# Start of a hybrid decoder block: how x is loaded, prepared and squared, and when the side work begins

## The chip, the core and the metric

The kernel runs on one core of a Trainium2 chip. The metric is the time of one execution in microseconds (us), as the device measures it; the median of several executions is compared. The core's engines are TensorE (PE, with its weight loads PEld), VectorE (DVE), ScalarE (ACT), GpSimd (POOL) and SyncE (SP); each works through its own list of instructions in order, and they wait for one another by semaphores. DMA transfers are issued by SP or ACT.

## What is computed

One decoder layer on 256 positions of width 2048, in fp32. What matters here is the beginning:

```python
h = rms_norm(x, g_mix)                 # x: (256, 2048)
proj = h @ w_in                        # 2048 x 8272; its columns are u, z_ssm, c_q, k, v, z_attn, ...
y_ssm = s5_branch(u, ...) * silu(z_ssm)  # S5: a scan over positions, on tables made from a, b, c, dt
...                                    # attention branch, gated merge, output projection, final norm
```

The row factor of the norm is taken out of the product: `proj = rstd * ((x * g_mix) @ w_in)`. So the products can start before the sum of squares of x is known, and the factor (`row1`) is applied when the sums are read from PSUM.

## The kernel before

**Units.** All weights come in 256 units of 128 x 1024 floats or less (512 KB). For each unit SP loads `raw` (5 buffers), ACT rounds it to `hi` (`unit_hi`, L252, 4 buffers), DVE takes `lo = raw - hi` (`unit_lo`, L264, 4 buffers), and PE multiplies: hi by the high part of the activations, hi by their low part, lo by their high part. A unit of the first 32 holds 8 blocks of 128 x 128 and makes 24 products of 256 columns. Units 0 to 3 are the first two blocks of u, woven: the first halves of both (x blocks 0 to 7), then the second halves (x blocks 8 to 15). They add up in one `aux` tile of PSUM, later blocks in `main` tiles (3 buffers).

**x.** x is loaded transposed, 16 blocks of 128 x 256 floats (2 MB), into `xT` (tile S). For each block ACT makes the high part (`xgh`, tile XH, L360) and DVE the low part (`xgl`, tile XL, L362). GpSimd squares blocks 0 to 7 and adds up most of the squares (L364, L368 to L370), ACT squares blocks 8 to 15 in one instruction (L367), DVE does the last two additions (L372, L373). From them come `rstd_cols` and `row1`.

**The main loop.** Step s issues the products of unit s on PE, then `unit_hi(s + 3)`, what was deferred to this step, `unit_lo(s + 2)`, the load of a further unit, and then `pump(1.3)`: the side work (generators, with costs in us) may spend 1.3 a step; what is not spent is kept up to 3.0. A generator that yields `("lag", n)` rests n steps. The framework then orders each engine's instructions by the order in the code and by an estimate of when they are ready, so an instruction may run somewhat before those written ahead of it.

**Side work of S5.** `s5_tables` (spawned with a lag of 3 steps) makes tables on DVE, GpSimd and PE. `s5_gen` starts when u (step 16) and the tables are there, and goes through two halves. Each half copies its input E from PSUM (ACT, L846), runs a long chain of DVE instructions on it (`cmadd`, L859 to L865), and at the end makes its output on PE (tile `aux`, 32 to 128 columns each). The first unit of c_q (step 104) has `need=["s5"]`: what is left of `s5_gen` is written out there, ahead of that unit's products. Steps 32 to 63 and 80 to 103 are units of 12 products of 512 columns, the others up to 104 of 24 products of 256.

**Beginning.** `first_loads` puts the gains, x and units 0 to 4 in one order on SP's queue. 18 products on a tile of zeros (`warm`) follow on PE. The first ACT instruction (`first`, L138) stands before all of this.

Of the kernel before, what the change touches and what calls it, by code (L numbers as in the profile page):

```python
# [12 lines left out]
AF = mybir.ActivationFunctionType  # L13
ALU = mybir.AluOpType
# [4 lines left out]
P = 128  # L19
T = 256  # L20
# [8 lines left out]
GA1 = 3  # L29
NC = 4  # L30
CW = 512
NWARM = 18
BUDGET = 1.3
XLAG = 1
ULATE = 4
TRLAG = 2

C_U, C_ZS, C_CQ, C_K, C_V, C_ZA, C_KI, C_GS, C_GA = 0, 1024, 2048, 2560, 2816, 3072, 4096, 4176, 6224
# [6 lines left out]
def block_kernel(ctx: ExitStack, tc: tile.TileContext, A: dict, out: bass.AP):  # L45
    nc = tc.nc
    V, S, G, PE = nc.vector, nc.scalar, nc.gpsimd, nc.tensor
    TT, STT = nc.vector.tensor_tensor, nc.vector.scalar_tensor_tensor
# [11 lines left out]
    def nm(s):  # L60
        uid[0] += 1
        return f"{s}_{uid[0]}"

    def slot(tag, shape, dt=F32):
        return cp.tile(shape, dt, tag=tag, name=nm(tag))

    def const(s, shape, dt=F32):
        return cp.tile(shape, dt, tag=s, name=s)
# [7 lines left out]
    def aux_ps():  # L76
        return pa.tile([P, 2, 512], F32, tag="aux", name=nm("aux"))
# [10 lines left out]
    def issue_unit(between=None):  # L88
        n = dma_next[0]
        if n >= len(units):  # L90
            return
        c, h, cols = units[n][:3]
        kind, idx = chunks[c]
        r = wp.tile([P, 1024], F32, tag="raw", name=nm("raw"), bufs=5)
        src = (A["wts"][idx] if kind == "w" else A["wvk"][idx])[:, h * cols:(h + 1) * cols]
        q = 2 if between else 1
        for i in range(q):
            s = slice(i * cols // q, (i + 1) * cols // q)
            nc.sync.dma_start(r[:, s], src[:, s])
            if between and i == 0:  # L100
                between()
        raws[n] = r
        dma_next[0] += 1
# [4 lines left out]
    gains = const("gains", [P, N_GAIN])  # L108
    xT = slot("S1", [P, KT, T])
    sabc = const("sabc", [P, 3, 32])  # L110

    def first_loads():
        def xload(k, n):
            nc.sync.dma_start(xT[:, k:k + n, :], A["xT"][:, k:k + n, :])

        nc.sync.dma_start(gains, A["gains"])
        xload(0, 2)
        issue_unit(lambda: xload(2, 2))
        xload(4, 4)
        issue_unit()  # L120
        xload(8, 4)
        xload(12, 4)
        for i in range(3):
            issue_unit()
        nc.sync.dma_start(sabc, A["sabc"])

    def gcol(base, i, p0=0, p1=P):
        return gains[p0:p1, base + i:base + i + 1]
# [6 lines left out]
    mhalf = const("mhalf", [P, 2])  # L135
    V.memset(mhalf, -0.5)
    first = const("first", [P, 2])
    S.activation(first, mhalf, AF.Copy)  # L138


    def mm(o, l, r, start=True, stop=True, **kw):
        PE.matmul(o, l, r, start=start, stop=stop, **kw)  # L142

    def mm3(o, wh, wl, ah, al, start, stop):
        mm(o, wh, ah, start=start, stop=False)
        mm(o, wh, al, start=False, stop=False)
        mm(o, wl, ah, start=False, stop=stop)
# [4 lines left out]
    def rstd_cols(sq, n, denom, tag, more=None):  # L152
        v = cp.tile([P, 2], F32, tag=tag + "_v", name=tag + "_v")
        if more is None:
            ps = small_ps()
            for t in range(2):
                mm(ps[:, 2 * t:2 * t + 2], sq[:n, t * P:(t + 1) * P], ones[:n, :])
            ss = ps[:, 0:4:2]
        else:
            ps = aux_ps()  # L160
            for m in (sq, more):
                for t in range(2):
                    mm(ps[:, t, 0:2], m[:n, t * P:(t + 1) * P], ones[:n, :], start=m is sq, stop=m is more)
            ss = ps[:, :, 0]
        V.tensor_scalar(v, ss, 1.0 / denom, EPS, ALU.mult, ALU.add)
        col = cp.tile([P, 2], F32, tag=tag + "_c", name=tag + "_c")
        G.tensor_tensor(col, v, mhalf, ALU.pow)
        return col
# [22 lines left out]
    def defer(n, fn):  # L191
        deferred.append((step[0] + n, fn))
# [14 lines left out]
    def spawn(gen, lag=0):  # L207
        t = [gen, step[0] + lag, False]
        threads.append(t)
        return t  # L210

    def spawn_first(gen):
        t = spawn(gen)
        threads.insert(0, threads.pop())
        return t
# [21 lines left out]
    def drain(t):  # L237
        while not t[2]:
            advance(t)
# [3 lines left out]
    def unit_hi(u):  # L243
        if u >= len(units):
            return
        cols = units[u][2]
        hi = wp.tile([P, 1024], F32R, tag="hi", name=nm("hi"))
        src = raws[u][:, :cols]
        q = 2 if u < 3 else 1
        for i in range(q):  # L250
            o = slice(i * cols // q, (i + 1) * cols // q)
            S.copy(hi[:, o], src[:, o])  # L252
        his[u] = hi
# [13 lines left out]
    def add_chunk(u0, u1, cols=1024, idx=None):  # L267
        c = len(chunks)
        if idx is None:
            n = sum(1 for k in chunks if k[0] == "w")  # L270
            chunks.append(("w", n))
        else:
            chunks.append(("v", idx))
        units.append((c, 0, cols) + u0)
        units.append((c, 1, cols) + u1)
# [1 line left out]
    def flush():  # L277
        run_deferred(True)

    def block_k16(act, evac, need=None, need1=None, M=P, acc=None, late=1):  # L280
        st = {}

        def go(h, hi, lo):
            ah, al = act()
            if h == 0:
                st["ps"] = (acc or main_ps)()
            ps = st["ps"]
            for k in range(8):
                kt = 8 * h + k
                mm3(ps[:M, :T], hi[:, k * M:(k + 1) * M], lo[:, k * M:(k + 1) * M], ah[:, kt, :], al[:, kt, :],  # L290
                    kt == 0, kt == 15)
            if h == 1:
                defer(late, lambda: evac(ps))
        return (lambda hi, lo: go(0, hi, lo), need), (lambda hi, lo: go(1, hi, lo), need1)
# [46 lines left out]
    R = {}  # L341
# [12 lines left out]

    xsq = slot("S2", [P, KT, T])

    def xprep(q):
        r = slice(4 * q, 4 * q + 4)
        for k in range(4 * q, 4 * q + 4):
            S.activation(xgh[:, k, :], xT[:, k, :], AF.Copy, scale=gcol(G_MIX, k))  # L360
        for k in range(4 * q, 4 * q + 4):
            STT(xgl[:, k, :], xT[:, k, :], gcol(G_MIX, k), xgh[:, k, :].bitcast(F32), ALU.mult, ALU.subtract)  # L362
        if q < 2:
            G.tensor_tensor(xsq[:, r, :], xT[:, r, :], xT[:, r, :], ALU.mult)  # L364

    def xnorm_gen():
        S.activation(xsq[:, 8:16, :], xT[:, 8:16, :], AF.Square)  # L367
        G.tensor_tensor(xsq[:, 0:4, :], xsq[:, 0:4, :], xsq[:, 4:8, :], ALU.add)  # L368
        G.tensor_tensor(xsq[:, 8:12, :], xsq[:, 8:12, :], xsq[:, 12:16, :], ALU.add)
        G.tensor_tensor(xsq[:, 0:4, :], xsq[:, 0:4, :], xsq[:, 8:12, :], ALU.add)  # L370
        yield ("lag", XLAG)
        TT(xsq[:, 0:2, :], xsq[:, 0:2, :], xsq[:, 2:4, :], ALU.add)  # L372
        TT(xsq[:, 0, :], xsq[:, 0, :], xsq[:, 1, :], ALU.add)  # L373
        yield 1.0
        yield ("lag", 1)
        R["col1"] = rstd_cols(xsq[:, 0, :], P, D, "r1")
        yield ("lag", 1)
        R["row1"] = row_of(R["col1"], "row1")
# [7 lines left out]
    def ev_u(nb):  # L386
        def f(ps):
            drain(R["xnorm"])
            TT(u[:, nb, :].rearrange("p (r j m) -> p r j m", r=2, j=4),
               ps[:, :T].rearrange("p (m j r) -> p r j m", j=4, r=2),  # L390
               R["row1"].rearrange("p (m j r) -> p r j m", j=4, r=2), ALU.mult)
            if nb == 7:
                R["s5"] = spawn(s5_gen(), 1)
        return f

    def late_x():
        xprep(2)
        xprep(3)
        R["xnorm"] = spawn_first(xnorm_gen())

    ua = {}

    def first_acc(nb):
        def f():
            if nb == 0:
                ua["ps"] = aux_ps()
            return ua["ps"][:, nb, :]
        return f

    for nb in range(8):  # L410
        first = nb < 2
        add_chunk(*block_k16(xact, ev_u(nb), need1=[late_x] if nb == 0 else None,
                             acc=first_acc(nb) if first else None, late=ULATE if first else 1))
        if nb == 1:
            weave()

# [671 lines left out]
    assert sum(1 for c in chunks if c[0] == "w") == NCH, (len(chunks), NCH)  # L1088


    R["s5t"] = spawn(s5_tables(), 3)
    first_loads()
    for i in range(NWARM):
        mm(wps[:, :T], warm[:, :P], warm)
    unit_hi(0)
    xprep(0)
    unit_lo(0)
    xprep(1)
    unit_hi(1)
    unit_lo(1)  # L1100
    unit_hi(2)
    NU = len(units)
    for s in range(NU):
        step[0] = s
        fn, need = units[s][3:]
# [129 lines left out]
```

## Time and profile before

| | us |
|---|---|
| median of 3 runs (lowest to highest) | 811.97 (811.44 to 812.96) |
| the profiled execution | 811.61 |
| its span, first to last instruction | 809.8 |
| PE busy in the span | 783.5 (97%) |
| DVE busy | 575.1 (71%) |
| ACT busy | 393.9 (49%) |
| GpSimd busy | 72.7 (9%) |

Times in the rows below are us from the start of the span, durations us if not marked ns. An engine that was idle carries in brackets how long it was, and what ended the wait. The granted clock (PEclk) is 1.00 at 2.4 GHz and 0.50 at 1.2 GHz.

### The profile page before, as it was taken

The numbers are of one execution on the slowest core, as the hardware profiler recorded it, in microseconds if no ns is written. First come the engines' busy times: TensorE is split into PE (matmuls) and PEld (weight loads), VectorE is DVE, ScalarE is ACT, GpSimd is POOL, SyncE is SP. The second block draws the span as 40 slices with busy tenths as digits, with TensorE's granted clock in tenths as the row PEclk, the third lists the DMA queues.
The fourth block names the chain that finished last, engine by engine and source line by source line (L and its number), as shares of the span: only waits on it lengthen the run. The fifth ranks groups of instructions, "written<-read, shape, count | busy, mean of one in ns | idle before, by whom it ended". The sixth has DMA issues, their size and how long they took to land.

```text
span 809.8 us, 12802 instructions
## 1 busy us (share of the span) xinstructions
PE 783.5 (97%) x5020; PEld 676.5 (84%) x5020; DVE 575.1 (71%) x834; ACT 393.9 (49%) x536; POOL 72.7 (9%) x77
## 2 busy tenths in 40 slices
PE   6899999999999999999999999999999999999993
PEld 5899997887999887799999987887887888888882
DVE  6999656999645999664669877666688555556662
ACT  6354544544566454463445474535445444445542
POOL 4369900000000000000000000000000000000000
PEclk7999999999999999999999999999999999999997
DMA  8576854656745655734754546676767665555522
GB/s 288 182 261 193 270 192 141 201 177 210 260 135 176 194 184 182 252 121 129 243 183 156 194 162 226 224 238 199 268 202 236 224 204 185 184 182 181 184 79 104
DMA packets 52061, 158.07 MB, mean 195 GB/s; under 512 B 5920, under 2 KB 12064, under 8 KB 51616
## 3 DMA queue, kind: packets, MB, share of 16 engines
q1 hardware_dynamic: 47392, 150.96, 57.2%
q10 hardware_dynamic: 4608, 6.29, 2.2%
q8 instruction: 39, 0.64, 0.3%
q14 instruction: 22, 0.18, 0.1%
HBM read 147.79 MB, written 8.39 MB: 193 GB/s over the span
## 4 chain that ended last, share of the span: by engine, by line
PE 36%; issue 11%; DMA 1%; DVE 1%; ACT 1%; ACTq 0%; POOLq 0%; POOL 0%; DVEq 0%
PE main L142 33%; PE aux L142 2%; PE aux L150 1%; DMA zld<-za_d 1%; DVE lo L264 0%; ACT hi L252 0%; DMA raw<-in_wts_dram 0%; DVE S L1022 0%; ACT S L1127 0%; ACTq L1230 0%; ACT S L586 0%; DVE t L980 0%; POOLq L1230 0%; POOL r_c L633 0%; ACT S L1023 0%
## 5 line engine op out<-in xcount | busy, mean ns | idle before, releaser
L252 ACT CAST hi<-raw 128x1024 fp32r<-128x1024 f32 (+2 forms) x259 | 266.4, 1031 | 363.7 <-PE main L142 318.3
L264 DVE TENSOR_TENSOR lo<-raw,hi 128x1024 fp32r<-128x1024 f32 (+2 forms) x259 | 316.5, 1225 | 154.6 <-ACT hi L252 154.0
L142 PE MATMUL main<-hi,S 128*128 128x512 f32 x544 | 175.3, 397 | 0.9 <-ACT S L1023 0.9
L142 PE MATMUL main<-hi,XH 128*128 128x512 f32 (+1 forms) x416 | 163.1, 392 | 0.0
L142 PE MATMUL main<-lo,XH 128*128 128x512 f32 (+1 forms) x416 | 162.4, 390 | 0.4 <-DVE lo L264 0.4
L142 PE MATMUL main<-hi,XL 128*128 128x512 f32 (+1 forms) x416 | 161.9, 389 | 0.0
L142 PE MATMUL main<-XH,hi 128*128 128x256 f32 x448 | 127.5, 285 | 0.0
L142 PE MATMUL main<-XH,lo 128*128 128x256 f32 x448 | 126.2, 282 | 0.0
L142 PE MATMUL main<-XL,hi 128*128 128x256 f32 x448 | 126.1, 282 | 0.0
L142 PEld LDWEIGHTS main<-hi,S 128*128 128x128 f32 x544 | 102.2, 188 | 25.2 <-ACT S L1023 1.6
L142 PE MATMUL main<-lo,S 128*128 128x512 f32 x272 | 107.9, 397 | 0.0
L142 PEld LDWEIGHTS main<-lo,XH 128*128 128x128 f32 x416 | 78.1, 188 | 18.8 <-DVE lo L264 1.9
L142 PEld LDWEIGHTS main<-hi,XH 128*128 128x128 f32 x416 | 78.1, 188 | 18.0
L142 PEld LDWEIGHTS main<-hi,XL 128*128 128x128 f32 x416 | 78.1, 188 | 17.3
L142 PEld LDWEIGHTS main<-XH,hi 128*128 128x128 f32 x448 | 84.8, 189 | 0.6
L142 PEld LDWEIGHTS main<-XH,lo 128*128 128x128 f32 x448 | 84.8, 189 | 0.0
L142 PEld LDWEIGHTS main<-XL,hi 128*128 128x128 f32 x448 | 84.7, 189 | 0.0
L142 PE MATMUL main<-S,hi 128*128 128x256 f32 x384 | 69.3, 283 | 0.1
L142 PEld LDWEIGHTS main<-S,hi 128*128 128x128 f32 x384 | 58.9, 188 | 1.7 <-issue 1.0
L142 PEld LDWEIGHTS main<-lo,S 128*128 128x128 f32 x272 | 51.2, 188 | 11.0
L142 PE MATMUL main<-S,lo 128*128 128x256 f32 x192 | 53.8, 280 | 0.0
L142 PEld LDWEIGHTS main<-S,lo 128*128 128x128 f32 x192 | 36.2, 188 | 0.0
(213 smaller groups left out, 687.0 us busy)
## 6 DMA issues: line engine op xcount, KB each, us to landing
raw<-in_wts_dram SPq DMA_DIRECT2D x247, 512.0 KB, 4.0
raw<-in_wvk_dram SPq DMA_DIRECT2D x8, 336.0 KB, 2.9
gs_d<-big ACTq DMA_DIRECT2D x8, 256.0 KB, 3.9
ga_d<-big ACTq DMA_DIRECT2D x8, 256.0 KB, 4.0
big<-gs_d SPq DMA_DIRECT2D x8, 256.0 KB, 4.3
big<-ga_d SPq DMA_DIRECT2D x8, 256.0 KB, 3.8
S<-in_grow_dram SPq DMA_DIRECT2D x2, 1024.0 KB, 7.7
big<-in_xtok_dram SPq DMA_DIRECT2D x8, 256.0 KB, 3.9
```

Of the source, the lines that this page charges most:

```text
L142: PE.matmul(o, l, r, start=start, stop=stop, **kw)
L150: PE.matmul(o, i, idn, is_transpose=True)
L252: S.copy(hi[:, o], src[:, o])
L264: TT(lo[:, o], src[:, o], his[u][:, o].bitcast(F32), ALU.subtract)
```

## The change

- x and the gains are loaded on ACT's queue, in order, and no longer between the units on SP's. Units 0 to 4 stand alone on SP's queue; two further units are issued ahead of the loop, so that the loop issues unit s + 7.
- GpSimd no longer works on x. ACT squares x in two instructions of 8 blocks (steps 2 and 3 of the loop), DVE adds all squares up (additions of 8, 4, 2 and 1 blocks, steps 4 and 5).
- The first two blocks (units 0 to 3) go by pass: 8 products of hi and high x, 8 of lo and high x, 8 of hi and low x, where each x block had its three products together.
- x is prepared in two groups of 8 blocks ahead of the loop; blocks 8 to 15 were prepared in step 2.
- 30 products on zeros in place of 18. The instruction `first` comes behind the loads.
- The first four blocks of u are read from PSUM later (6, 5, 3 and 2 steps after their last unit in place of 4, 4, 1 and 1).
- `xnorm_gen` is spawned ahead of the loop with a lag of 2; `s5_tables` starts with a lag of 7 steps in place of 3.

```diff
-NWARM = 18
+NWARM = 30
...
-            nc.sync.dma_start(xT[:, k:k + n, :], A["xT"][:, k:k + n, :])
-
-        nc.sync.dma_start(gains, A["gains"])
+            nc.scalar.dma_start(xT[:, k:k + n, :], A["xT"][:, k:k + n, :])
+
+        nc.scalar.dma_start(gains, A["gains"])
         xload(0, 2)
-        issue_unit(lambda: xload(2, 2))
+        xload(2, 2)
         xload(4, 4)
-        issue_unit()
         xload(8, 4)
         xload(12, 4)
-        for i in range(3):
+        issue_unit(lambda: None)
+        for i in range(4):
             issue_unit()
         nc.sync.dma_start(sabc, A["sabc"])
...
-            for k in range(8):
+            if split:
+                for i, (w, a) in enumerate(((hi, ah), (lo, ah), (hi, al))):
+                    for k in range(8):
+                        kt = 8 * h + k
+                        mm(ps[:M, :T], w[:, k * M:(k + 1) * M], a[:, kt, :], start=kt == 0 and i == 0,
+                           stop=kt == 15 and i == 2)
+            for k in range(0 if split else 8):
...
     def xnorm_gen():
-        S.activation(xsq[:, 8:16, :], xT[:, 8:16, :], AF.Square)
-        G.tensor_tensor(xsq[:, 0:4, :], xsq[:, 0:4, :], xsq[:, 4:8, :], ALU.add)
-        G.tensor_tensor(xsq[:, 8:12, :], xsq[:, 8:12, :], xsq[:, 12:16, :], ALU.add)
-        G.tensor_tensor(xsq[:, 0:4, :], xsq[:, 0:4, :], xsq[:, 8:12, :], ALU.add)
-        yield ("lag", XLAG)
-        TT(xsq[:, 0:2, :], xsq[:, 0:2, :], xsq[:, 2:4, :], ALU.add)
-        TT(xsq[:, 0, :], xsq[:, 0, :], xsq[:, 1, :], ALU.add)
-        yield 1.0
+        for h in range(2):
+            S.activation(xsq[:, 8 * h:8 * h + 8, :], xT[:, 8 * h:8 * h + 8, :], AF.Square)
+            yield ("lag", 1)
+        for n in (8, 4, 2, 1):
+            TT(xsq[:, 0:n, :], xsq[:, 0:n, :], xsq[:, n:2 * n, :], ALU.add)
+            yield 1.0
         yield ("lag", 1)
...
-        first = nb < 2
-        add_chunk(*block_k16(xact, ev_u(nb), need1=[late_x] if nb == 0 else None,
-                             acc=first_acc(nb) if first else None, late=ULATE if first else 1))
+        add_chunk(*block_k16(xact, ev_u(nb), acc=first_acc(nb) if nb < 2 else None,
+                             late=(6, 5, 3, 2)[nb] if nb < 4 else 1, split=nb < 2))
...
-    R["s5t"] = spawn(s5_tables(), 3)
+    R["xnorm"] = spawn(xnorm_gen(), 2)
+    R["s5t"] = spawn(s5_tables(), 7)
     first_loads()
+    S.activation(first, mhalf, AF.Copy)
     for i in range(NWARM):
         mm(wps[:, :T], warm[:, :P], warm)
     unit_hi(0)
-    xprep(0)
+    xhi(range(8))
     unit_lo(0)
-    xprep(1)
+    xlo(range(8))
     unit_hi(1)
     unit_lo(1)
     unit_hi(2)
+    xhi(range(8, 16))
+    xlo(range(8, 16))
+    for i in range(2):
+        issue_unit()
```

## Rows read from the trace of the kernel before

**Rows 1.** The page, busy time by engine: us, share of the span, instructions

```profile
PE 783.5 (97%) x5020; PEld 676.5 (84%) x5020; DVE 575.1 (71%) x834; ACT 393.9 (49%) x536; POOL 72.7 (9%) x77
```

**Rows 2.** Timeline of PE, 0 to 45: start, us, what [idle before <-releaser]

```profile
1.04 4.02 PE L142 MATMUL main<-warm 128*128 128x256 bf16 x18 [1.04 <-DVE mhalf L136]
...
15.32 0.58 PE L142 MATMUL aux<-XL,hi 128*128 128x256 f32 x1 [1.49 <-DVE XL L362]
...
24.15 0.27 PE L142 MATMUL main<-XL,hi 128*128 128x256 f32 x1
27.52 0.39 PE L142 MATMUL aux<-XH,lo 128*128 128x256 f32 x1 [3.09 <-DVE lo L264]
...
31.11 0.42 PE L142 MATMUL aux<-XH,lo 128*128 128x256 f32 x1
31.32 0.41 PE L142 MATMUL main<-XH,lo 128*128 128x256 f32 x1
...
32.33 0.28 PE L142 MATMUL main<-XL,hi 128*128 128x256 f32 x1
...
33.75 0.28 PE L142 MATMUL main<-XL,hi 128*128 128x256 f32 x1
```

**Rows 3.** Windows: stretch, busy us by engine (instructions), then PEclk, DMA share, GB/s

```profile
8.36:18.59 10.23, 6.30 (x24) 5.42 (x25) 8.88 (x13) 8.67 (x18) 4.33 (x3) 0.50 0.95 355
...
28.84:32.25 3.41, 3.41 (x19) 3.41 (x18) 3.15 (x6) 0.90 (x1) 0.00 (x0) 0.50 0.83 267
...
10.00:15.00 5.00, 1.74 (x5) 1.01 (x4) 4.56 (x3) 4.45 (x11) 4.31 (x2) 0.50 1.01 392
```

**Rows 4.** Timeline of DVE, 0 to 45

```profile
11.09 4.97 DVE L362 SCALAR_TENSOR_TENSOR XL<-S,gains,XH 128x256 fp32r<-128x256 f32 x4 [0.44 <-ACT XH L360]
...
17.19 3.24 DVE L362 SCALAR_TENSOR_TENSOR XL<-S,gains,XH 128x256 fp32r<-128x256 f32 x8
...
24.08 4.52 DVE L264 TENSOR_TENSOR lo<-raw,hi 128x1024 fp32r<-128x1024 f32 x2
...
29.12 1.21 DVE L264 TENSOR_TENSOR lo<-raw,hi 128x1024 fp32r<-128x1024 f32 x1
```

**Rows 5.** Timeline of GpSimd, 0 to 45

```profile
10.59 1.89 POOL L364 TENSOR_TENSOR S<-S 128x1024 f32<-128x1024 f32 x1 [2.22 <-DMA S<-in_xT_dram]
...
19.40 4.51 POOL L369 TENSOR_TENSOR S<-S 128x1024 f32<-128x1024 f32 x1 [4.42 <-ACT S L367]
```

**Rows 6.** Timeline of ACT, 0 to 45

```profile
0.72 1.28 ACT L138 ACT_TABLE_LOAD   x1 [0.72 <-PEq L1224]
...
13.19 3.30 ACT L360 ACTIVATE XH<-S,gains 128x256 fp32r<-128x256 f32 x8
...
17.42 1.91 ACT L367 ACTIVATE S<-S 128x2048 f32<-128x2048 f32 x1
```

**Rows 7.** Timeline of SP's queue, 0 to 45

```profile
3.06 0.43 SPq L114 DMA_DIRECT2D S<-in_xT_dram  x1
3.53 0.43 SPq L99 DMA_DIRECT2D raw<-in_wts_dram  x1
```

**Rows 8.** DMA issues at 3.06 and 3.53: count, KB, us from issue to landing

```profile
S<-in_xT_dram SPq DMA_DIRECT2D x1, 512.0 KB, 7.5
...
raw<-in_wts_dram SPq DMA_DIRECT2D x1, 512.0 KB, 8.3
```

**Rows 9.** Timeline of DVE: begin and end of the second S5 half's chain

```profile
259.45 1.23 DVE L859 TENSOR_TENSOR S<-S,pre 128x1024 f32<-128x1024 f32 x1 [0.57 <-ACT S L846]
...
331.80 4.83 DVE L264 TENSOR_TENSOR lo<-raw,hi 128x1024 fp32r<-128x1024 f32 x4
```

**Rows 10.** Windows: the stretch of that chain, columns as in rows 3

```profile
260.00:330.00 70.00, 69.79 (x338) 57.42 (x337) 69.21 (x100) 30.89 (x32) 0.00 (x0) 1.00 0.58 189
```

**Rows 11.** Timeline of PE: that half's input (E), and its output at step 104

```profile
256.58 1.16 PE L142 MATMUL aux<-S,S 64*128 64x128 f32 x16
...
337.02 0.64 PE L142 MATMUL aux<-S,S 128*32 128x128 f32 x16
```

More of the change, by code (lines that the diff above doesn't have):

```diff
@@ L31 @@
 CW = 512
-NWARM = 18
+NWARM = 30
 BUDGET = 1.3
-XLAG = 1
-ULATE = 4
 TRLAG = 2
@@ L137, in block_kernel @@
     first = const("first", [P, 2])
-    S.activation(first, mhalf, AF.Copy)
     def mm(o, l, r, start=True, stop=True, **kw):
@@ L278, in flush, with block_k16 @@
         run_deferred(True)
-    def block_k16(act, evac, need=None, need1=None, M=P, acc=None, late=1):
+    def block_k16(act, evac, need=None, need1=None, M=P, acc=None, late=1, split=False):
         st = {}
@@ L355, in block_kernel, with xhi, xlo @@
     xsq = slot("S2", [P, KT, T])
-    def xprep(q):
-        r = slice(4 * q, 4 * q + 4)
-        for k in range(4 * q, 4 * q + 4):
+    def xhi(ks):
+        for k in ks:
             S.activation(xgh[:, k, :], xT[:, k, :], AF.Copy, scale=gcol(G_MIX, k))
-        for k in range(4 * q, 4 * q + 4):
+    def xlo(ks):
+        for k in ks:
             STT(xgl[:, k, :], xT[:, k, :], gcol(G_MIX, k), xgh[:, k, :].bitcast(F32), ALU.mult, ALU.subtract)
-        if q < 2:
-            G.tensor_tensor(xsq[:, r, :], xT[:, r, :], xT[:, r, :], ALU.mult)
     def xnorm_gen():
-        S.activation(xsq[:, 8:16, :], xT[:, 8:16, :], AF.Square)
-        G.tensor_tensor(xsq[:, 0:4, :], xsq[:, 0:4, :], xsq[:, 4:8, :], ALU.add)
-        G.tensor_tensor(xsq[:, 8:12, :], xsq[:, 8:12, :], xsq[:, 12:16, :], ALU.add)
-        G.tensor_tensor(xsq[:, 0:4, :], xsq[:, 0:4, :], xsq[:, 8:12, :], ALU.add)
-        yield ("lag", XLAG)
-        TT(xsq[:, 0:2, :], xsq[:, 0:2, :], xsq[:, 2:4, :], ALU.add)
-        TT(xsq[:, 0, :], xsq[:, 0, :], xsq[:, 1, :], ALU.add)
-        yield 1.0
+        for h in range(2):
[4 more added lines that the diff above has]
+            yield 1.0
         yield ("lag", 1)
@@ L394, in ev_u @@
         return f
[L396 to L399, printed above, removed]
     ua = {}
```

## The prediction, made before the result was known

> **What bounds the kernel now.** I read the page first: PE is busy for 97% of the span [rows 1], so only what makes PE idle or slow counts. Next the timeline of PE by idle time. The holes lie in the first 33 us, and in the tail after the last product, which the change doesn't touch. At the start PE stands again and again for x, the last time until 15.32, and once for 3.09 us on `lo` [rows 2]. The windows add a second loss: the granted clock is 0.50 (1.2 GHz) from 8.36 to 18.59 and from 28.84 to 32.25 [rows 3], each time behind a stretch in which PE had mostly stood; it rose at 18.59 after PE had run unbroken from 15.32.
>
> To put both losses in one number: at 32.33 the clock is high and the 104th real product begins (96 of units 0 to 3, over at 31.11; of the fifth unit two near 24.15 and five from 31.32). From there products begin (33.75 - 32.33) / 12 = 0.118 us apart [rows 2]. An unbroken run at that pace would have begun at 32.33 - 103 x 0.118 = 20.2. This is the start to beat.
>
> The timelines of DVE and GpSimd tell why `lo` was late: four XL beside GpSimd's squares took 4.97 us, where eight later ones took 3.24, and two `lo` beside its addition took 4.52, where one alone takes 1.21 [rows 4, 5].
>
> **The change part by part: the start.** x and weights go out on two queues at once. Of the first 2 MB (x blocks 0 to 7, units 0 and 1) before's order let x blocks 4 to 7 land at 3.06 + 7.5 = 10.56, and unit 1, the last of them, at 3.53 + 8.3 = 11.83 [rows 7, 8]. No row shows two queues loading together here, so these two are the bounds for x blocks 4 to 7: its old place, or an even share with the weights, which puts it at the end of the 2 MB. I take the middle, 11.2.
>
> The Trainium skill ("DMA: Bandwidth & Descriptors", section "Queues, rings and completion order") says that each DMA engine takes turns between the queues that have work, a packet at a time. By it 11.8 is right, x comes later than before and 0.6 us is lost against my sum; no run here shows it yet.
>
> On ACT six issues of some 0.45 (SP's took 0.43 [rows 7]) delay the table load of 1.28 [rows 6] from 0.72 to about 3.4, so ACT is free near 4.9. That is before most of x lands: hidden.
>
> ACT needs 3.30 / 8 = 0.41 for a block [rows 6], so blocks 4 to 7 end at 11.2 + 1.65 = 12.85, and the first pass of unit 0 with them. Its other 16 products then have their operands (XL at 3.24 / 8 = 0.40, now without GpSimd). The clock will be low again, because PE stands between the warm-up and 11.2; at 0.21 a product (31.11 to 31.32 [rows 2]) they take 3.4, to 16.25. By then PE has run unbroken for 3.4 us, as it had for 3.3 when the clock rose at 18.59. Unit 1 follows at full pace; its `hi` is ready near 14. That is 24 products at 16.25, a start of 16.25 - 24 x 0.118 = 13.4. **Gain: 20.2 - 13.4 = 6.8.** If x lands at 11.83 and the clock rises only at 18.6, it is 5.3. If it lands at 10.56 and the compiler fills the wait with second and third passes of blocks 0 to 3 (8 products, 1.7), it is 9.
>
> Later needs: unit 2 begins at 16.25 + 24 x 0.118 = 19.1. The second 2 MB at 392 GB/s [rows 3] land 5.1 after 11.2, at 16.3, and ACT's last four blocks are done at about 18.2. Just in time.
>
> Costs elsewhere: 12 more warm-up products follow 18 that took 4.02 [rows 2]; at 0.118 to 0.22 they end between 6.5 and 7.7, while PE still waits for x. ACT squares 8 more blocks (1.91 [rows 6]) and DVE adds 8 and 4 blocks more (1.21 for 1024 columns [rows 4], so at most 2.4 + 1.2 = 3.6). `lo` takes 1.21 of a unit's 2.84, so in steps 4 to 9 this and the readings of u fit, but the small S5 work slips behind them. The later readings of u hold no buffer that is missed: the third `main` buffer is free, and block 5, which reuses that of block 2, starts at step 10, two steps after it is read. The earlier units on SP's queue wait for the same buffers as before: nothing.
>
> **The change part by part: the tables.** They seem free, as they fill DVE's idle time, but they set when S5 reaches PE. I counted credits. Before, the tables start at step 3 with 3.0 saved, lose 1.0 to the squares, and need 23.7 up to the powers: 3.0 - 1.0 + 1.3 x 17 first reaches it in step 20. After, the squares take 4.0 in steps 4 and 5 and the start at step 7 finds 2.9: 2.9 + 1.3 x 16 = 23.7, step 23. All behind it is lags and the same budget, so every later piece comes 3 steps later: the last products of E of the second half in step 78, not 75.
>
> Before, those stand at 256.58 [rows 11], DVE's chain on them begins at 259.45, and the four `lo` behind its last instruction begin at 331.80 [rows 9]. In between DVE is busy for 69.21 of 70 us [rows 10], so the chain cannot be squeezed. PE takes up its result at 337.02, at step 104 [rows 11], which does not move. Slack: 5.2. Three units of 24 products are 3 x 2.84 = 8.5. So E comes 8.5 later against PE, and PE stands for **8.5 - 5.2 = 3.3** ahead of the output; behind it are the whole queue of PE and then `hi`, which waits for PE's buffers. From below: nothing, if the compiler lays unit 104's products ahead of the output. From above: three more `lo` inside the chain (3.6), and a low clock afterwards. From 28.84 to 32.25, behind the 3.09 us wait, this cost 3.41 / 0.21 = 16 products x 0.095 = 1.5 [rows 2, 3]. Together 8.4. I take 3.3, since both orders of the `lo` seen here keep the chain at its length.
>
> **Sum.** The profiled execution took 811.61: 811.61 - 6.8 + 3.3 = 808.1. The median of the runs is 0.36 above it: **808.5 us**.
>
> **The rivals.**
> *A, as above:* 6.8 gained, some 3 given back at step 104; 807 to 810.5. For it: the saturated chain. Against it: only the compiler's order.
> *B, nothing given back:* PE fills the wait with unit 104, or the chain comes in time; 811.97 - 6.8 = 805.2, with the start's upper bound 803. For it: at 24.15 the compiler had put two products of the fifth unit ahead of the fourth's [rows 2]. Against it: before, it had laid four `lo` behind the chain's end [rows 9], so it judged the output ready early.
> *C, the change does not do what it says at the start:* x gains no speed by a second queue, ACT's list stands behind the second half of unit 0, or XH of blocks 12 to 15 is late for unit 2. Then some 3 to 4 are gained and 3.3 given back: 811.5 to 812.3.
> *D, slower:* the same wait at step 104, with the `lo` of units 103 to 105 ahead of the chain's end and the clock low after it: 8.4 lost against 6.8, 813.6. It decides once the wait with its clock is over 6.8.
>
> **How the numbers follow.** A 0.45, B 0.27, C 0.18, D 0.10. The measurement tells about 0.2%, 1.6 us, from no change. Faster than 810.3: A but for 0.03, all of B, 0.03 of C: 0.72. Slower than 813.6: half of D, 0.01 of C, and 0.02 for a stall that I have not seen: 0.08. The same: 0.20. The range reaches from the middle of B to the middle of C: 804.4 to 812.0, which leaves out 0.04 of B, 0.05 of C and D.
>
> **What would show it.** Right: real products unbroken from about 13, the clock at 2.4 GHz from about 16, the 104th product near 13.4 + 103 x 0.118 = 25.6 in place of 32.33; no XL or `lo` above 1.3 in the first 40 us; near 330 a wait of PE of about 3 us in front of aux products, released by DVE's chain (L865), with E's last products 3 units later than before. Wrong: x blocks 4 to 7 after 12, a second low clock before 30, PE going on with c_q's first unit ahead of the S5 output (B), or any PE wait on `lo` in steps 4 to 10, where DVE has 3.6 us more to do.

## The result, and the profile of the changed kernel

The changed kernel took 818.7 us (median of 4 runs, 816.27 to 819.09) against 812.47 of before beside it: ratio **1.0069, 95% interval 1.0042 to 1.0095**. It is 0.7% slower; 808.5 was forecast. The profiled execution took 816.27 us, its span is 814.5. It is the shortest of the four: the other three took 818.5 to 819.1, at a mean granted clock of 0.981 to 0.983 against its 0.986.

The page of the changed kernel, busy time as in [rows 1], and all waits of PE above 3 us (total, times, longest):

```profile
PE 786.5 (97%) x5032; PEld 678.6 (83%) x5032; DVE 575.5 (71%) x836; ACT 398.0 (49%) x539; POOL 58.3 (7%) x72
```
```profile
PE main L139 <- DVE lo L261: 5.1, 3, 4.5
PE aux L139 <- DVE S L859: 3.5, 1, 3.5
PE aux L139 <- ACT XH L362: 3.4, 2, 2.9
```

The engines' shares have hardly moved, but for GpSimd's. The waits have: those on XL and the one on `lo` of the start are gone, one on `lo` stands at a new place, and one on DVE's S (the S5 chain) is new. Where they lie, in PE's timeline, as in [rows 2] and [rows 11]:

```profile
1.04 6.24 PE L139 MATMUL main<-warm 128*128 128x256 bf16 x30 [1.04 <-DVE mhalf L134]
10.18 1.78 PE L139 MATMUL aux<-XH,hi 128*128 128x256 f32 x4 [2.89 <-ACT XH L362]
...
17.28 1.11 PE L139 MATMUL aux<-XH,hi 128*128 128x256 f32 x8
...
26.63 0.28 PE L139 MATMUL main<-XL,hi 128*128 128x256 f32 x1
...
63.43 0.58 PE L139 MATMUL main<-XH,lo 128*128 128x256 f32 x1 [4.54 <-DVE lo L261]
...
342.99 0.65 PE L139 MATMUL aux<-S,S 128*32 128x128 f32 x16 [3.46 <-DVE S L859]
```

The 104th product on x begins at 26.63 (32.33 before [rows 2]): the start did gain, 5.7. The wait at 342.99 is the one forecast for step 104. The one at 63.43 was not foreseen. To see what each is worth I counted the products on x in the traces and took the time at which the nth begins (us; one trace each; the last two columns are kernels of the experiments):

| product | before | after | after - before | e13 | e15 |
|---|---|---|---|---|---|
| 104th | 32.33 | 26.63 | -5.70 | 24.24 | 24.02 |
| 120th | 34.22 | 28.52 | -5.70 | 26.13 | 25.91 |
| 360th | 63.51 | 58.38 | -5.13 | 56.93 | 56.38 |
| 480th | 77.71 | 79.89 | +2.18 | 71.13 | 70.58 |
| 768th | 116.85 | 118.16 | +1.31 | 110.28 | 109.77 |
| 1152nd | 212.08 | 214.84 | +2.76 | 205.16 | 204.66 |
| last on PE | 796.28 | 800.33 | +4.05 | 788.68 | 789.03 |

From the 120th to the 480th 7.9 us are lost, more than the whole gain. The windows of that stretch (columns as in [rows 3]), first of the changed kernel, then of the one before, and the changed kernel's timeline of DVE in it, shortened to what takes long:

```profile
61.41:68.24 6.83, 4.81 (x22) 4.81 (x23) 6.83 (x5) 0.00 (x0) 6.83 (x5) 0.50 0.42 131
40.00:60.00 20.00, 18.71 (x156) 18.29 (x155) 19.90 (x35) 8.01 (x10) 14.26 (x11) 1.00 0.31 106
60.00:80.00 20.00, 16.54 (x118) 16.31 (x119) 20.00 (x16) 4.45 (x4) 19.43 (x19) 0.83 0.43 131
```
```profile
40.00:60.00 20.00, 20.00 (x172) 20.00 (x171) 19.86 (x50) 10.22 (x12) 12.24 (x17) 1.00 0.76 265
60.00:80.00 20.00, 20.00 (x171) 20.00 (x171) 19.15 (x20) 9.17 (x10) 18.88 (x25) 1.00 0.62 185
```
```profile
46.04 1.91 DVE L677 TENSOR_TENSOR sp_exc<-sp_nr,sabc 128x32 f32<-128x32 f32 x1
...
55.66 2.37 DVE L677 TENSOR_TENSOR fre<-sp_exc,sp_x 128x32 f32<-128x32 f32 x1
...
59.62 2.61 DVE L763 TENSOR_TENSOR S<-S,fre 128x1024 f32<-128x1024 f32 x1
62.15 1.22 DVE L261 TENSOR_TENSOR lo<-raw,hi 128x1024 fp32r<-128x1024 f32 x1
...
65.66 3.39 DVE L763 TENSOR_TENSOR S<-S,fre 128x1024 f32<-128x1024 f32 x1
```

DVE is busy all the time and does less: 35 and 16 instructions in the two windows of 20 us (before 50 and 20, with PE busy for 20.00 in each). An instruction on 32 columns takes 2.37, and one on 1024 columns takes 3.39, where the `lo` at 62.15 takes 1.22. GpSimd's timeline shows what runs beside them, in the changed kernel and in the one before:

```profile
45.94 1.96 POOL L769 TENSOR_TENSOR S<-S,abar 128x1024 f32<-128x1024 f32 x1
...
54.51 3.48 POOL L771 TENSOR_TENSOR S<-S,S 128x1024 f32<-128x1024 f32 x1
...
64.61 3.35 POOL L771 TENSOR_TENSOR S<-S,S 128x1024 f32<-128x1024 f32 x1
```
```profile
83.67 1.92 POOL L775 TENSOR_TENSOR S<-S,abar 128x1024 f32<-128x1024 f32 x1
...
98.03 2.41 POOL L777 TENSOR_TENSOR S<-S,S 128x1024 f32<-128x1024 f32 x1
```

GpSimd's share of the S5 tables is a long list of powers on 32 columns and six products on 1024 columns (`cmul_g`). Before, the six stood at the end of the powers, at 83.67 to 100.4. Now they stand among them, at 45.94 to 68.0, beside DVE's own products for the tables. DVE's 2.37 from 55.66 ends where GpSimd's 3.48 from 54.51 ends (58.0). DVE's 3.39 from 65.66 ends 1.1 behind the end of GpSimd's 3.35 from 64.61, about the time of one such instruction. The Trainium skill ("SBUF — State Buffer", section "SBUF: two separate sides") says that DVE and GpSimd share a pair of ports which the one that starts first holds for a whole instruction, and that DVE's operations with two SBUF inputs take part in this against GpSimd's that read SBUF. The rows agree (1.21 with GpSimd idle [rows 3, 4], 3.39 beside it).

### The profile page after: what moved, and what is told of

The parts are those of the page before. It is cut to its first block, busy times and chain, and to the rows that moved or that the text cites. A ratio compares the mean times of both kernels' runs of the same rounds, so it can differ in the third digit from the quotient of the medians.

```text
span 814.5 us, 12825 instructions
## 1 busy us (share of the span) xinstructions
PE 786.5 (97%) x5032; PEld 678.6 (83%) x5032; DVE 575.5 (71%) x836; ACT 398.0 (49%) x539; POOL 58.3 (7%) x72
## 4 chain that ended last, share of the span: by engine, by line
PE 37%; issue 11%; ACT 1%; DVE 1%; ACTq 0%; POOLq 0%; POOL 0%
PE main L139 34%; PE aux L139 2%; PE aux L147 1%; DVE lo L261 0%; ACT hi L249 0%; DVE S L1016 0%; ACT S L1127 0%; ACTq L1230 0%; ACT S L580 0%; POOLq L1230 0%; POOL r_c L627 0%; ACT S L1017 0%; DVE t L974 0%; PE small L147 0%; DVE r_v L625 0%
## 5 line engine op out<-in xcount | busy, mean ns | idle before, releaser
L261 DVE TENSOR_TENSOR lo<-raw,hi 128x1024 fp32r<-128x1024 f32 (+2 forms) x259 | 309.6, 1199 | 164.2 <-ACT hi L249 163.7
```

Of the source, the lines that this page charges most:

```text
L261: TT(lo[:, o], src[:, o], his[u][:, o].bitcast(F32), ALU.subtract)
```

## The experiments

The landmarks are of one profile each. The same start code gave the 104th product at 25.61, 25.88 and 24.02 in three kernels (e5, e10, e15), so differences of the 104th product under 2 us are not read. Between experiments the ratios to the kernel before, measured beside each, are the safer comparison.

**e1: hold GpSimd's large products behind the powers.** The changed kernel with

```diff
-            G.tensor_scalar(psi[:, i, 0], psi[:, i, 1], -1.0, None, ALU.mult)
+            R["lastpow"] = G.tensor_scalar(psi[:, i, 0], psi[:, i, 1], -1.0, None, ALU.mult)
...
-        cmul_g(ct[:, 0, 1], ct[:, 0, 0], ci[:, 0], abr, abi, ALU.subtract)
-        cmul_g(ct[:, 1, 1], ct[:, 0, 0], ct[:, 1, 0], nabi, abr, ALU.add)
+        with tc.issue_after(R["lastpow"].ins):
+            cmul_g(ct[:, 0, 1], ct[:, 0, 0], ci[:, 0], abr, abi, ALU.subtract)
+            cmul_g(ct[:, 1, 1], ct[:, 0, 0], ct[:, 1, 0], nabi, abr, ALU.add)
```

> The changed kernel with one thing undone: GpSimd's six large table instructions (128x1024) are held behind its 49 small power instructions, as they ran before the change. Theory T1 (they run 35 us earlier now and block DVE's two-tensor instructions between 46 and 68 us, so lo comes late and PE stands and falls to 1.2 GHz): the 4.5 us wait of PE on lo near 59 and the low clock after it vanish, 818.7 falls by 5 to 8 to 811 to 813. Rival R1 (DVE simply has too much to do there, because the sums of squares, the readings of u and the small S5 work were pushed together): the wait stays, less than 2 us change.

Measured 810.11, ratio 0.9964 (0.9952 to 0.9976): 8.6 below the changed kernel. GpSimd's products are back behind 84, and in the timeline of DVE `lo` beside them takes up to 3.13, without a wait of PE. GpSimd's first product, that `lo`, and the two largest waits of PE in the whole run, neither of them on `lo`:

```profile
84.42 1.92 POOL L769 TENSOR_TENSOR S<-S,abar 128x1024 f32<-128x1024 f32 x1
```
```profile
98.70 3.13 DVE L261 TENSOR_TENSOR lo<-raw,hi 128x1024 fp32r<-128x1024 f32 x1 [0.54 <-ACT hi L249]
```
```profile
PE aux L139 <- ACT XH L362: 4.2, 2, 3.7
PE aux L139 <- DVE S L860: 3.5, 1, 3.5
```

That `lo` had waited 0.54 for `hi` before it began: DVE has time to spare there. So the collision costs about 8 us where DVE has none, and nothing later.

**e2: start the tables as early as before.** The changed kernel with

```diff
-            yield 1.0
+            yield 0.25
...
-    R["s5t"] = spawn(s5_tables(), 7)
+    R["s5t"] = spawn(s5_tables(), 3)
```

> The changed kernel with the side work's credits as before: tables spawned with a lag of 3 steps, the four additions of squares charged 0.25 each and not 1.0, so that the second S5 half starts in step 72 again and not in step 75. Theory T2 (the 3.5 us wait of PE at step 104 is those 3 steps): that wait is gone, 818.7 falls by 3 to 4 to about 815, the wait near 59 stays or grows by 1 or 2. Rival R2 (the wait at step 104 comes from DVE's delay earlier, in the collision): it stays at 2 us or more.

Measured 817.22, 1.0046 (1.0032 to 1.006). The wait at step 104 went, but PE stood 2.3 for "issue" in the same place, and once for 2.4 on the reading of u (L389). GpSimd's products stayed early (from 41.71), and so did the waits on `lo` (3.9). So the early start alone does not undo the collision, and the fall of 3 to 4 did not come.

**e3: both of these.** Edits of e1 and e2.

> Both of these together: GpSimd's large table instructions behind the powers, and the credits as before. T1 and T2: only the gain of the start is left, about 5.7 us of the profiled execution: 806 to 808. If either rival holds, 810 or more.

Measured 810.52, 0.9967 (0.9954 to 0.998): not better than e1, and not the 806 to 808 of both theories. PE's "issue" hole is there again (1.6), and a wait of 1.3 on the reading of u.

**e4: the queue alone.** The kernel before with

```diff
-            nc.sync.dma_start(xT[:, k:k + n, :], A["xT"][:, k:k + n, :])
+            nc.scalar.dma_start(xT[:, k:k + n, :], A["xT"][:, k:k + n, :])
...
-        nc.sync.dma_start(gains, A["gains"])
+        nc.scalar.dma_start(gains, A["gains"])
```

> The kernel before with one part of the change alone: gains and x are loaded on ACT's queue. T1 in its full form (it is this part that lets the table loads go out early and so turns GpSimd's order round): GpSimd's large table instructions start before 50 us, and a wait of PE on lo of 2 us or more appears between 45 and 75; the time is 812.5 plus 2 to 6, or less if x lands sooner. Rival R3 (the queue alone is harmless, the collision needs the later tables too): no PE wait above 0.5 us after 35, time within 2 us of 812.5.

Measured 823.56, 1.0127 (1.0113 to 1.0141), more than any theory had. GpSimd's products came early here too (from 46.37), with waits of PE on `lo` of 3.2 between 46 and 75 and the granted clock low from 64.50 to 67.91. A part of the loss lies ahead of them: PE stands 3.29 until 37.08 in front of its products for the sum of squares, and the clock is low from 37.19 to 44.02. The 104th product came at 30.91, no sooner than can be told.

**e5: all but the queue.** e1 with x, the gains and the first units back on SP's queue, as before:

```diff
-            nc.scalar.dma_start(xT[:, k:k + n, :], A["xT"][:, k:k + n, :])
+            nc.sync.dma_start(xT[:, k:k + n, :], A["xT"][:, k:k + n, :])
...
```

> Like e1 (large GpSimd instructions behind the powers), with one more part undone: gains, x and units 0 to 4 in one order on SP's queue, as before the change. Theory T3 (the queue move itself costs at the start: x blocks 4 to 7 share the engines with the weights and land at 11.9 and not 10.6, and ACT, which issues x, is held by its fourth and fifth issue until 7.2): x blocks 4 to 7 are there by 10.6, the 104th product comes 1 to 2 us sooner than e1's 27.44, the time is 1 to 2 below e1's 810.1. Rival R4 (two queues bring x sooner, as the change means it): 104th product later than 27.5, time 1 or more above e1.

Measured 806.87, 0.9935 (0.992 to 0.995), 3.2 below e1 (2.4 by the ratios). ACT's timelines tell why, first of the changed kernel, then of e5 (ACTq is ACT issuing DMAs):

```profile
1.17 5.99 ACTq L112 DMA_DIRECT2D S<-in_xT_dram  x5
7.19 1.28 ACT L1088 ACT_TABLE_LOAD   x1 [7.19 <-DMA S<-in_xT_dram]
...
11.92 1.71 ACT L362 ACTIVATE XH<-S,gains 128x256 fp32r<-128x256 f32 x4 [0.60 <-DMA S<-in_xT_dram]
```
```profile
0.72 1.28 ACT L1089 ACT_TABLE_LOAD   x1 [0.72 <-PEq L1225]
...
10.00 1.70 ACT L362 ACTIVATE XH<-S,gains 128x256 fp32r<-128x256 f32 x4 [0.62 <-DMA S<-in_xT_dram]
```

With x on its queue ACT issues until 7.16, so its first XH begins at 9.62 (4.48 in e5), and x blocks 4 to 7 are there at 11.92, against 10.00.

**e7: without the order by pass.** e1 with `split` off:

```diff
-                             late=(6, 5, 3, 2)[nb] if nb < 4 else 1, split=nb < 2))
+                             late=(6, 5, 3, 2)[nb] if nb < 4 else 1))
```

> Like e1, with one part undone: units 0 to 3 not by pass, but three products for each x block in turn. T: the passes let PE run 8 products while lo and XL are still being made; without them the start loses 0.3 to 1.5 us (104th product after 27.7), time 810.3 to 811.6. Rival (with GpSimd off x, XL is quick enough, so the order of the products is worth nothing): within 0.5 us of e1.

Measured 808.94, 0.9957 (0.9943 to 0.9971): no worse than e1. The order by pass gains nothing that can be told.

**e8: GpSimd at work on x again.** e1 with GpSimd's squares of blocks 0 to 7 and its three large additions:

```diff
+    for r in (slice(0, 4), slice(4, 8)):
+        G.tensor_tensor(xsq[:, r, :], xT[:, r, :], xT[:, r, :], ALU.mult)
...
```

> Like e1, with one part undone: GpSimd squares x blocks 0 to 7 and does the three large additions again, DVE only the last two. T: XL and lo of the first 20 us are held up beside GpSimd (1.2 to 3 us each in place of 0.4 and 1.2), the 104th product comes 3 to 6 us later than e1's 27.44, time 813 to 816. Rival (the price lies in the order and the warm-up, not in GpSimd): less than 1.5 us.

Measured 816.21, 1.0051 (1.0036 to 1.0065), 6 above e1 (7 by the ratios). In the timeline of DVE the eight XL that take 3.25 elsewhere take 7.00:

```profile
12.22 7.00 DVE L366 SCALAR_TENSOR_TENSOR XL<-S,gains,XH 128x256 fp32r<-128x256 f32 x8
```

**e9: e5 with e2's early tables.**

> Like e5 and with the credits as before (e3's edit: tables with a lag of 3, squares charged 0.25). By T3 and by what e3 showed (the wait of 3.5 us at step 104 goes, but 1.6 us of issue come in its place and 1.3 us on the reading of u): 0 to 2 below e5, 807 to 809.5. If the wait at step 104 was hidden anyway: same as e5 within 0.5.

Measured 806.94, 0.9934 (0.9919 to 0.9949), the same as e5. The wait at step 104 is gone, and a hole of the same place has its time (PE's timeline):

```profile
337.95 0.69 PE L139 MATMUL aux<-S,S 128*32 128x31 f32 x30 [2.40 <-issue]
```

**e10: is the hold needed without the queue?** e5 without e1's hold, which is the changed kernel but for the queue.

> The changed kernel with x, the gains and the units back on SP's queue in the old order; GpSimd's large table instructions are not held back by hand. Theory: the collision comes only from the tables' loads sb and sc going out early because x is off SP's queue; then these loads go out near 40 again, GpSimd's 128x1024 instructions lie behind the powers (after 80 us), PE has no wait on lo above 1 us, and the time is that of the kernel with x on SP's queue and the hold, 807 (0.9935, 0.991 to 0.996). Rival: the order of GpSimd's list is set by the tables' later start or by the new squares, whichever queue x is on; then the waits on lo near 60 stay and the time is 814 to 816.

Measured 815.03, 1.0019 (1.0000 to 1.0038): the theory fell (the 12 runs took 808.0 to 816.0; why so far apart is open). The products come early again, and PE waits on `lo`, though the first table load goes out at 30.01, not near 10:

```profile
47.09 1.96 POOL L769 TENSOR_TENSOR S<-S,abar 128x1024 f32<-128x1024 f32 x1
```
```profile
PE main L139 <- DVE lo L261: 3.8, 3, 2.6
```

So x off SP's queue is one trigger, and something else is another.

**e11 and e12: 18 warm-up products; no order by pass.** Both are e5 with one edit each, `NWARM = 18` and `split` off as in e7.

> x on SP's queue, GpSimd's large instructions held behind the powers, and 18 warm-up products in place of 30. Theory: the warm-up products fill a stretch in which PE would only wait for x (the first real product begins at 7.08 right behind them), and the clock falls all the same before 10.5; so the time is the same, 807 (0.992 to 0.995), with the 104th product at 25.6 within 0.3. Rival 1: the twelve more products hold the clock up over the first real ones; without them it falls earlier and the 104th product comes 0.5 to 1.5 us later, 807.5 to 808.5. Rival 2: they delay the first products; without them the 104th comes up to 1 us sooner.

> x on SP's queue, GpSimd's large instructions held behind the powers, and the first two blocks of u in the old order, each x block's three products together. Theory: the order by pass is worth nothing, as on ACT's queue (1.2 us sooner without it there, near what can be told): 805.5 to 807.5 (0.991 to 0.9945), the 104th product between 24.5 and 26. Rival: with x landing earlier the pass order matters, because the lo and XL of the first half are late; then the 104th product comes after 26.5 and the time is 808 or more.

Measured 807.66, 0.994 (0.9924 to 0.9956), and 807.07, 0.993 (0.9911 to 0.9948): e5's 0.9935 both. Neither part is worth anything that these runs can tell (the intervals reach 1.3 to 1.5 us to either side).

**e13: GpSimd off x alone.** The kernel before with

```diff
-        if q < 2:
-            G.tensor_tensor(xsq[:, r, :], xT[:, r, :], xT[:, r, :], ALU.mult)
...
+        for h in range(2):
+            S.activation(xsq[:, 8 * h:8 * h + 8, :], xT[:, 8 * h:8 * h + 8, :], AF.Square)
+            yield ("lag", 1)
+        for n in (8, 4, 2, 1):
+            TT(xsq[:, 0:n, :], xsq[:, 0:n, :], xsq[:, n:2 * n, :], ALU.add)
+            yield 1.0
```

> The kernel before with one part of the change alone: GpSimd no longer works on x (ACT squares x in two instructions of 8 blocks, DVE adds all squares up, in the steps where the old squares were spawned); x stays on SP's queue, the tables start at step 3, the first two blocks keep their order. Theory: freeing GpSimd of x is what gains at the start (the four XL beside it fall from 4.97 to about 1.7, the lo pair from 4.52 to 2.4, the wait of 3.09 on lo goes; the 104th product at 27 to 29.5 in place of 32.33), and it also pulls GpSimd's 128x1024 table instructions in among the powers, ahead of 80 us; beside them lo takes 2.4 to 3.4 and PE waits on lo between 60 and 95; sum 808 to 813 (0.995 to 1.0). Rival 1: the start gains as much and the large instructions, wherever they run, meet idle time of DVE: no wait on lo above 0.5, 806.5 to 808.5 (0.990 to 0.995). Rival 2: without the other parts the start gains nothing, because ACT's longer squares or DVE's four additions delay lo as much as GpSimd did: 812 or more (1.0 and above).

Measured 805.65, 0.9913 (0.9896 to 0.9929), the first rival (by the ratio; the time is 0.9 below its range). One part of the change, by itself, gains more than any kernel so far: the 104th product comes at 24.24, 8.1 sooner. GpSimd's products do come among the powers, but from 77.36 on, where DVE waits for `hi` between the `lo` (timelines of GpSimd and DVE, and the longest wait of PE on `lo`):

```profile
77.36 1.92 POOL L771 TENSOR_TENSOR S<-S,abar 128x1024 f32<-128x1024 f32 x1
...
93.98 2.39 POOL L773 TENSOR_TENSOR S<-S,S 128x1024 f32<-128x1024 f32 x1
```
```profile
94.02 3.43 DVE L264 TENSOR_TENSOR lo<-raw,hi 128x1024 fp32r<-128x1024 f32 x1 [2.42 <-ACT hi L252]
```
```profile
PE aux L142 <- DVE lo L264: 0.2, 1, 0.2
```

**e14 and e15: the tables' start.** e14 is e13 with the late start; e15 is e10 with the early one (the squares' costs stay 1.0):

```diff
e14: -    R["s5t"] = spawn(s5_tables(), 3)
e14: +    R["s5t"] = spawn(s5_tables(), 7)
e15: -    R["s5t"] = spawn(s5_tables(), 7)
e15: +    R["s5t"] = spawn(s5_tables(), 3)
```

> The kernel before with GpSimd off x and the tables' start 7 steps late in place of 3; nothing else. Theory: the late start is what draws GpSimd's 128x1024 table instructions into the stretch from 45 to 85 in which DVE has no idle time (with it DVE's products for the tables and the readings of u come together); PE then waits on lo there for 3 to 5, with a low clock after it, and of the 7 to 8 gained by GpSimd off x alone (0.9913) nearly all is lost: 811 to 815 (0.998 to 1.003). Rival: the late start does no harm in this kernel, the collision came from the by-pass order or from x's two preparations ahead of the loop: 804 to 807 (0.990 to 0.994), no wait on lo over 0.5.

> The changed kernel with x, gains and units back on SP's queue and the tables' start 3 steps late as before; nothing is held by hand. Against the run of 1.0019, which differs by the start at 7 steps alone. Theory: with the earlier start GpSimd's large instructions come behind 75, no wait on lo above 0.5 between 40 and 80, and the time is that of the kernels with the hold, 806 to 808.5 (0.992 to 0.9955). Rival: the large instructions come early again, whatever the start: 812 or more (0.999 and above).

e14 took 815.89 (12 runs, 811.1 to 818.1), 1.0033 (1.0013 to 1.0054); e15 took 803.88, **0.9893 (0.988 to 0.9906)**, the fastest of all and below the range of its theory. One number, 3 or 7, is worth 1.2 to 1.3% in both (1.0033 to 0.9913, 1.0019 to 0.9893). GpSimd's timeline and PE's waits in e14, then GpSimd's timeline and PE's holes at step 104 in e15:

```profile
46.23 1.93 POOL L771 TENSOR_TENSOR S<-S,abar 128x1024 f32<-128x1024 f32 x1 [0.57 <-DMA S<-in_sc_dram]
```
```profile
PE main L142 <- DVE lo L264: 5.2, 2, 3.4
PE aux L142 <- DVE S L861: 3.5, 1, 3.5
```
```profile
73.43 2.90 POOL L769 TENSOR_TENSOR S<-S,abar 128x1024 f32<-128x1024 f32 x1
```
```profile
330.44 0.65 PE L139 MATMUL aux<-S,S 128*32 128x128 f32 x16 [0.56 <-DVE S L859]
...
336.85 0.69 PE L139 MATMUL aux<-S,S 128*32 128x96 f32 x31 [0.70 <-issue]
```

With x on SP's queue the late start brings both losses: the collision, and the wait at step 104. In e14 and e10 the collision comes a little later than in the changed kernel: the clock is low from 72.97 to 79.79 and from 75.49 to 82.31. e15 against e13 (0.9893, 0.9913) holds all other parts of the change together: 1.6 us, with intervals that overlap.

## Why the prediction was wrong

**The step that failed** is that of the tables: "They seem free, as they fill DVE's idle time, but they set when S5 reaches PE." I followed their start through the credits to step 104, and did not ask what it does to the order of GpSimd's list; the sum has no term for it. Six large products of GpSimd moved from 83.67 to 45.94, into a stretch in which DVE has no idle time. That costs 8.6 (e1 against the changed kernel); with the products held back the kernel takes 0.9964 of before, near the forecast (808.5 to 811.97 is 0.9957). e14 and e15 show the late start itself as a trigger. In the changed kernel the queue is another: undoing the start alone (e2) or the queue alone (e10) leaves the collision, undoing both (e15) removes it. Why the framework's order comes out so is not shown, nor whether the late start would do it with GpSimd still at work on x. The rows of GpSimd that I read ended at 45; its table products of before, at 83.67, were not among them, and no term or rival had them. My sign for "wrong" named a PE wait on `lo`, but in steps 4 to 10 and for DVE's additions; it came ahead of the 363rd product, in unit 15.

**A second step failed beside it:** "six issues of some 0.45 ... hidden". ACT was held for 5.99, not some 2.5, and its table load began at 7.19, not 3.4. The queue costs 2.4 to 3.2 (e1 against e5), and it triggers the collision as well (e4): with x gone from SP's queue the first table load goes out at 9.72 (10.05 in e4, 40.42 before), and GpSimd's products are early in each kernel of this kind without the hold. SP's queue, in the changed kernel and before:

```profile
9.72 0.43 SPq L752 DMA_DIRECT2D S<-in_sb_dram  x1
```
```profile
40.42 0.43 SPq L758 DMA_DIRECT2D S<-in_sb_dram  x1
```

A part that I had counted in the start's gain is a loss.

**The start's gain** was 5.7 against 6.8 forecast, within the bounds of 5.3 to 9 and nearer than such a landmark tells; the clock rose at 17.04 where 16.25 was taken. The middle taken for x blocks 4 to 7 (11.2) was too early: they are there at 11.92, the bound of an even share (11.83), which is worth 0.7 in the prediction's sum. The Trainium skill's rule of turns by packet ("DMA: Bandwidth & Descriptors", section "Queues, rings and completion order") had given 11.8; the run agrees with it. What gains is GpSimd off x alone: 8.1 at the 104th product (e13), 6 to 7 us by e8. The forecast did read that from [rows 4] (the addition beside the two `lo` of 24.08 is one at 23.99, not the one shown in [rows 5]), but counted the queue, the order and the warm-up products along with it.

**Step 104** was right in kind and size: 3.46 for 3.3 forecast, E's last products come behind 1512 products on x, 1440 before, which is the three units forecast (267.86, against 256.58):

```profile
267.86 1.16 PE L139 MATMUL aux<-S,S 64*128 64x128 f32 x16
```

What it is worth in time is less plain. The kernel before has an "issue" hole of 1.59 inside that output, which the sum did not count and which is not seen where PE has waited 3.5 ahead of it. From the 1152nd product to the last on PE it takes 584.2 before, 585.5 in the changed kernel, 587.1 in e5, 586.2 in e9 and 584.4 in e15. In e5 and e9 the granted clock is low for 3.4 us there, behind the wait (334.57 to 337.98) and behind the hole of 2.40 (338.52 to 341.94); in the other three it stays at 1.00. So e9 gains little over e5, and most of e15's 3.4 against e5 (0.9893 to 0.9935) is this place: a wait of 0.56 and a hole of 0.70, with the clock at 1.00.

**The rivals.** D had the sign and a low clock after a wait, but at another place. C's own terms (4 gained, 3.3 given back) begin at 811.3, not 811.5. For the sum: 811.61 - 5.7 + 7.9 leaves 813.8; from the 480th product on another 1.9 is lost (4.05 - 2.18): 815.7. The profiled execution took 816.27; the other 0.6 lies behind PE's last product. The median, 818.7, is 2.4 higher; where that is lost no profile shows.

## What to carry to other kernels

When side work is moved in time, follow each engine that it uses, not only the queue on which its result is awaited: a late start can push one engine's long instructions beside another's tight stretch. Price a collision by the idle time of the engine that is hit: the same 3.4 us instructions cost 8 us at 60 and nothing at 95. Try the parts of a bundle one by one: here a single one was worth 0.9% alone, and two others, a queue and a start, turned it into a loss.

## What the runs showed of the hardware beyond what was expected

- Five x loads held ACT for 5.99 us (1.17 to 7.16), where SP's take 0.43 each [rows 7]. The first three go out one behind the other; the fourth goes out at 4.19 and the fifth at 6.82. Each waits for the semaphore of an earlier load: the gains (issued at 0.72, landed 3.5 later) and the first x load (issued at 1.17, landed 5.6 later). So the issuing engine stands until a load of its own has landed.
- PE's "issue" hole inside the output of step 104 is 0.22 to 2.42 long in the kernel before, e2, e3, e4, e9, e13 and e15, which do not wait long ahead of it; none is seen there in the kernels that wait 3.5. What it is, and whether the wait hides it, was not tried.
- A granted clock of 1.00 in a window can mean that nothing is recorded there. In the trace of e13 the records of the clock begin at 13.43 (4.94 in the kernel before, 23.54 in e4), and the window ahead of that reads 1.00 (columns as in [rows 3]). PE's timeline shows the products 0.21 apart up to 13.23 and 0.11 to 0.12 from 13.45 on, the paces that go with 0.50 and 1.00 in [rows 2, 3]: the clock was low up to there.

```profile
10.00:13.20 3.20, 3.20 (x14) 2.97 (x14) 2.94 (x6) 3.20 (x6) 0.00 (x0) 1.00 1.03 401
```
```profile
13.02 0.42 PE L142 MATMUL aux<-XH,hi 128*128 128x256 f32 x1
13.23 0.37 PE L142 MATMUL aux<-XL,hi 128*128 128x256 f32 x1
13.45 0.28 PE L142 MATMUL aux<-XH,lo 128*128 128x256 f32 x1
13.56 0.28 PE L142 MATMUL aux<-XH,hi 128*128 128x256 f32 x1
```
